# Reading the second layer's expert tokens by indirect transfers and fp32 transposes instead of one-hot matmuls

## The chip, the cores and the metric

The kernel runs on one core of one Trainium2 chip. The time is that of one execution on the device, in microseconds (us), from the first to the last instruction on the slowest (here the only) core, with the launch around it. What counts is the median of several executions.

## The reference, cut to what matters

The model is a trunk of two layers over 256 latent and 256 context tokens of 1024 numbers, all in fp32. A layer is a mixing part (state space, attention, matrix memory) and then a mixture of 64 experts. The first layer's experts see all 512 tokens, the second layer's the 256 latent ones. Each token goes to 8 experts, whose outputs are added with a gate:

```
_, top_e = lax.top_k(jnp.where(allowed, biased, -jnp.inf), TOP_K)      # 8 of 64
gate = jnp.take_along_axis(scores, top_e, axis=1)
gate = gate / jnp.sum(gate, -1, keepdims=True) * ROUTED_SCALE
...
def expert_block(acc, blk):
    tok, g, e = blk                       # 128 rows of one expert
    xb = h[tok]                           # the tokens of this expert
    ob = (jax.nn.silu(xb @ w_gate[e]) * (xb @ w_up[e])) @ w_down[e]
    return acc.at[tok].add(ob * g[:, None]), None
...
shared = (jax.nn.silu(h @ sw_gate) * (h @ sw_up)) @ sw_down
return routed + shared
```

w_gate and w_up are 1024 x 256 for each expert, w_down is 256 x 1024. The line `xb = h[tok]` is the one whose carrying out is changed, in the second layer alone. So 256 x 8 = 2048 token rows are read there.

## The kernel before

`moe(l, ...)` runs a layer's experts. `choose` and `route` find each token's experts, sort the experts by their number of tokens (an expert's place in that order is its rank) and leave the experts' numbers in `idt`. `experts` (from L1634 on in the listing) is a generator that walks through *units*. A unit is one or two tiles of 128 rows: kinds B, C and X have two tiles, and the kinds that the end of the stage is made of have one tile shared by several experts (S: four experts with 32 rows each; M: two with 64). Each expert's part of a tile is a segment. Layer 2 has 26 units with 32 tiles, in the fixed order BDMCSMSLXLMSCXDSCSSSMSLMSM.

Weights come through `ring`, 18 slots of 512 KB in layer 2; an expert takes six of them. `load` (L1720, on SyncE's queue) fills a slot as soon as `use` has given it back. A load of an expert without tokens is skipped once the ring has gone round; 12 of 64 experts have none here, and they come late in the order.

For unit i, `experts` emits: `gather(units[i+2])`, `gate_up(unit i)` (8 steps of matmuls `gu`, L1785), the gate function, `transp(units[i+1])`, `down(units[i-1])` (matmuls `dn`, L1798), the turning of the hidden values (`hT`), and `slots(units[i+5])`. A scheduler then sets the order on each engine, so that the transposes of unit i+1 fall among the first `gu` matmuls of unit i.

`slots` builds one-hot matrices `oneh` (token x place in the tile, bf16), and with matmuls over them finds the token number `gi`/`si` and the gate `gc` of every place. `transp` must give `xT`, the tile's tokens with the 1024 numbers along the partitions, in eight blocks of 128 x 128. In layer 1 `gather` reads the rows of the tokens from `fd` in DRAM by one indirect transfer per segment on GpSimd's queue into one of five tiles `xg`, and `transp` turns them by eight fp32 transposes (`tpose`, L290). In layer 2 there is no gather: `parts` (L1452) has split the normalised tokens f into three bf16 parts `fb` per token tile whose sum is f, and `transp` multiplies each part of both token tiles with the one-hot matrix: 2 x 3 = 6 matmuls per block, 48 per tile (L1760).

`down` scales the outputs by the gates into `xo` (4 buffers) and adds them to `Y` in DRAM by an indirect transfer per segment on GpSimd's queue (L1808). As they add to the same memory, each waits until the one before has landed. The last unit is not scattered: `fold` adds it by matmuls. Afterwards `combine` reads Y back (`cat<-Y`) and forms the output.

Of the kernel before, what the change touches and what calls it, by code (L numbers as in the profile page):

```python
# [20 lines left out]
D = 1024  # L21
# [228 lines left out]
class Trunk:  # L250
    def __init__(self, ctx, tc, d, dbg=None):
# [17 lines left out]
        self.x2 = self.dram.tile([NT, D], F32, name="x2d")  # L269
        self.fd = self.dram.tile([TOK[0], D], F32, name="fd")  # L270
        self.Y = [self.dram.tile([TOK[l] + 128, D], F32, name=f"Y{l}") for l in range(DEPTH)]
# [1083 lines left out]
    def post(self, l, cat, pp, mq, fT, sw):  # L1355
# [38 lines left out]
        def norm(at):  # L1394
            i = tiles[at]
            m = 0 if i >= 2 else 1
            xt = xts[i]
            t = pp.tile([128, D], F32, name="pt", bufs=2)
            for n in range(2):
                cs = slice(n * 512, (n + 1) * 512)  # L1400
                v.tensor_tensor(out=t[:, cs], in0=st[at][n], in1=g1[m][:, cs], op=OP.mult)
            sums = pp.tile([128, 2], F32, name="sums", bufs=2)
            v.scalar_tensor_tensor(out=t, in0=xt, scalar=ALPHA, in1=t, op0=OP.mult, op1=OP.add, accum_out=sums[:, 0:1])
            x1 = pp.tile([128, D], F32, name="x1", bufs=2)
            self.ln_rows(x1, t, *self.ln_sums(pp, t, sums[:, 0:1], x1, "p"), gn, bs, accum_out=sums[:, 1:2])
            nc.sync.dma_start(self.x1[l][i * 128:(i + 1) * 128, :], x1)
            f = pp.tile([128, D], F32, name="f", bufs=2)
            nm, rs = self.ln_sums(pp, x1, sums[:, 1:2], f, "p2")
            v.scalar_tensor_tensor(out=f, in0=x1, scalar=nm, in1=sc[m], op0=OP.add, op1=OP.mult)
            v.scalar_tensor_tensor(out=f, in0=f, scalar=rs, in1=sh[m], op0=OP.mult, op1=OP.add)  # L1410
            if not last:
                nc.sync.dma_start(self.fd[at * 128:(at + 1) * 128, :], f)
            st[at] = f
            if at + 2 < len(tiles):
                fetch(tiles[at + 2])
# [13 lines left out]
        nt = len(tiles)  # L1429
        self.fb = {}  # L1430
        self.G, self.pos1 = (mq.tile([128, nt, 64], F32, name=n) for n in ("G", "pos1"))
# [6 lines left out]
        for at in range(nt):  # L1438
# [8 lines left out]
            self.choose(l, at, lg, pp)  # L1447
            if last:
                self.parts(at, st[at], pp, mq)
        return lg, tiles  # L1450

    def parts(self, i, f, pp, mq):  # L1452

        nc, v = self.nc, self.nc.vector
        fb = self.fb[i] = mq.tile([128, 3, D], BF16, name=f"fb{i}")
        r = pp.tile([128, D], F32, name="frest", bufs=2)
        nc.scalar.copy(fb[:, 0], f)
        v.tensor_tensor(out=r, in0=f, in1=fb[:, 0], op=OP.subtract)
        nc.scalar.copy(fb[:, 1], r)
        v.tensor_tensor(out=r, in0=r, in1=fb[:, 1], op=OP.subtract)  # L1460
        nc.scalar.copy(fb[:, 2], r)

# [117 lines left out]
    def slots(self, l, units, rp, mq):  # L1580
# [6 lines left out]
        for u in units:  # L1587
            for t in u["tiles"]:
                segs = t["segs"]
                n, rk, m = len(segs), sorted(x[0] for x in segs), max(x[2] + x[3] for x in segs)  # L1590
                by = slice(rk[0], rk[-1] + 1, rk[1] - rk[0] if n > 1 else 1)
                t["oh"] = oh = rp.tile([128, nt, 128], BF16, name="oneh", bufs=12 if l else 3)
                lot = [segs] if [x[0] for x in segs] == rk and len({x[1:4:2] for x in segs}) == 1 else [[x] for x in segs]
# [98 lines left out]
    def experts(self, l, units, mq, rp, ring, merge):  # L1692
# [41 lines left out]
        def gather(u):  # L1734
            if l:
                return
            for t in u["tiles"]:
# [3 lines left out]
                for (_, _, col, _, cap), si in zip(t["segs"], t["si"]):  # L1741
                    nc.gpsimd.indirect_dma_start(out=x[col:col + cap], out_offset=None, in_=self.fd,  # L1742
                                                 in_offset=bass.IndirectOffsetOnAxis(ap=si[0:cap], axis=0),
                                                 bounds_check=TOK[l] - 1, oob_is_err=False)

        def transp(u):
            for t in u["tiles"]:
                m = t["m"]
                xt = self.xtp.tile([128, 8, 128], F32, name="xT", bufs=4)
                for hh in range(2):  # L1750
                    ps = self.bank("xT")
                    for k in range(4):
                        cs = slice((hh * 4 + k) * 128, (hh * 4 + k + 1) * 128)
                        o = ps[:, k * 128:k * 128 + m]
                        if l == 0:
                            self.tpose(o, t["x"][0:m, cs])
                        else:
                            parts = [(i, z) for i in self.fb for z in range(3)]
                            for at, (i, z) in enumerate(parts):
                                nc.tensor.matmul(o, self.fb[i][:, z, cs], t["oh"][:, i, 0:m], start=at == 0, stop=at + 1 == len(parts))  # L1760
                    o, a = xt[:, hh * 4:hh * 4 + 4, 0:m], ps.rearrange("p (k n) -> p k n", k=4)[:, :, 0:m]
# [157 lines left out]
    def moe(self, l, mq, fT, sw, lg, tiles, spare):  # L1919
# [5 lines left out]
        with ExitStack() as es:  # L1925
            rp = es.enter_context(self.tc.tile_pool(name=f"moe{l}", bufs=1))
            if l == 0:
                self.xg = [rp.tile([128, D], F32, name=f"xg{i}") for i in range(5)]
                for x in self.xg:
                    nc.gpsimd.memset(x, 0.0)  # L1930
            ring = rp.tile([128, 18 if last else 13, 1024], F32, name="ring")
# [101 lines left out]
```

## Time and profile before

| what | value |
|---|---|
| median of 3 runs | 1990.86 us (1983.97 to 1991.81) |
| the profiled execution | 1989.93 us |
| its span, from first to last instruction | 1988.1 us |
| busy in the span: TensorE, VectorE, ScalarE, GpSimd | 91%, 41%, 19%, 23% |
| DMA | 524.16 MB, 264 GB/s on average |
| layer 2's expert matmuls | from 1440.74 to 1947.76 us |

In the page, PE is TensorE, DVE VectorE, ACT ScalarE, POOL GpSimd and SP SyncE. The chain of waits is the work that ended last, followed back from the end; a row of it has its start, its length and what ran (or what was waited for). A DMA share is the mean busy share of the core's 16 DMA engines; it can come out a little over 1. The group of a line gives busy time and the mean length of one instruction; matmuls overlap in the pipeline, so the mean can be longer than the busy time divided by the count.

### The profile page before, as it was taken

The numbers are of one execution on the slowest core, as the hardware profiler recorded it, in microseconds if no ns is written. First come the engines' busy times: TensorE is split into PE (matmuls) and PEld (weight loads), VectorE is DVE, ScalarE is ACT, GpSimd is POOL, SyncE is SP. The second block draws the span as 40 slices with busy tenths as digits, with TensorE's granted clock in tenths as the row PEclk, the third lists the DMA queues.
The fourth block names the chain that finished last, engine by engine and source line by source line (L and its number), as shares of the span: only waits on it lengthen the run. The fifth ranks groups of instructions, "written<-read, shape, count | busy, mean of one in ns | idle before, by whom it ended". The sixth has DMA issues, their size and how long they took to land. (4 is left out here: it accounts for less than half of the span.)

```text
span 1988.1 us, 29110 instructions
## 1 busy us (share of the span) xinstructions
PE 1802.0 (91%) x10161; PEld 851.0 (43%) x10161; DVE 813.2 (41%) x2298; ACT 379.5 (19%) x739; POOL 456.1 (23%) x453
## 2 busy tenths in 40 slices
PE   6998999879999999899997178899899999999992
PEld 2554665523334333233332055665543354433340
DVE  6856664731223432222121598764731222312113
ACT  2245331201111111001111313341301011110000
POOL 3120211232223232332221551002101211111223
PEclk7999999989999999999999588999999999999996
DMA  8442567399999999999997423256499999899672
GB/s 321 140 96 101 178 250 293 116 319 358 298 326 340 360 323 293 386 377 339 344 297 232 163 75 64 75 213 258 182 372 343 398 353 358 304 385 355 234 261 69
DMA packets 153922, 524.16 MB, mean 264 GB/s; under 512 B 28787, under 2 KB 37939, under 8 KB 145068
## 3 DMA queue, kind: packets, MB, share of 16 engines
q1 hardware_dynamic: 135228, 480.36, 65.1%
q0 software_dynamic: 18544, 41.90, 9.5%
q8 instruction: 82, 1.34, 0.3%
q14 instruction: 68, 0.56, 0.1%
HBM read 531.12 MB, written 47.61 MB: 291 GB/s over the span
## 5 line engine op out<-in xcount | busy, mean ns | idle before, releaser
L1785 PE MATMUL gu<-ring,xT 128*32 128x512 f32 (+5 forms) x2896 | 645.7, 602 | 18.2 <-DMA ring<-in_exp_w 17.7
L1785 PEld LDWEIGHTS gu<-ring,xT 128*32 128x32 f32 (+5 forms) x2896 | 193.7, 129 | 399.3 <-issue 321.2
L1798 PE MATMUL dn<-ring,hT 128*32 128x512 f32 (+5 forms) x1448 | 330.0, 597 | 4.8 <-DMA ring<-in_exp_w 4.0
L1808 POOL DMA_INDIRECT Y<-xo,gi x79 | 119.9, 1518 | 610.8 <-DMA Y<-xo,gi 140.5
L1681 DVE TENSOR_TENSOR hh<-gu,sg 128x256 f32<-128x256 f32 (+4 forms) x86 | 36.5, 424 | 523.2 <-ACT sg L1680 503.7
L1798 PEld LDWEIGHTS dn<-ring,hT 128*32 128x32 f32 (+5 forms) x1448 | 103.1, 128 | 183.2 <-issue 155.7
L1808 POOL DMA_INDIRECT Y<-xo,si x66 | 91.0, 1379 | 302.6 <-DMA Y<-xo,gi 217.4
L1803 DVE TENSOR_SCALAR xo<-dn,gc 128x512 f32<-128x512 f32 (+5 forms) x80 | 60.0, 751 | 229.0 <-PE dn L1798 215.6
L1680 ACT ACTIVATE sg<-gu 128x256 f32<-128x256 f32 (+4 forms) x86 | 32.8, 384 | 586.6 <-PE gu L1785 586.3
L443 PE MATMUL pT<-hT,w 128*128 128x512 f32 (+1 forms) x288 | 120.4, 572 | 4.3 <-DMA w<-in_w_mm 2.7
L1760 PEld LDWEIGHTS <-fb 128*128 128x128 bf16 x1536 | 86.3, 99 | 41.9 <-issue 41.9
L1802 ACT ACTIVATE xo<-dn,gc 128x512 f32<-128x512 f32 (+5 forms) x80 | 55.0, 687 | 253.3 <-PE dn L1798 239.2
L1760 PE MATMUL xT<-oneh,fb 128*128 128x128 bf16 (+4 forms) x1536 | 94.6, 220 | 0.0
L1392 PE MATMUL yo<-w,cat 128*128 128x512 f32 x192 | 83.4, 594 | 0.8 <-DMA w<-in_w_out 0.8
L1762 DVE COPY xT<-xT 128x512 f32<-128x512 f32 (+5 forms) x80 | 53.2, 670 | 70.0 <-PE xT L1760 37.2
L1762 ACT COPY xT<-xT 128x512 f32<-128x512 f32 (+5 forms) x80 | 45.8, 573 | 185.4 <-PE xT L1760 135.3
L443 PEld LDWEIGHTS pT<-hT,w 128*128 128x128 f32 x288 | 56.0, 200 | 58.0 <-issue 47.5
L290 PE MATMUL hT<-cst,xt 128*128 128x128 f32 x64 | 14.6, 404 | 59.3 <-ACT xt L1982 55.2
L451 PE MATMUL pN<-w,hT 128*128 128x256 f32 (+2 forms) x256 | 65.0, 414 | 3.0 <-DVE va L1268 3.0
L342 PE MATMUL ada<-w,sil 128*32 128x512 f32 x384 | 57.9, 649 | 10.4 <-DMA w<-in_ada_w 10.4
L1742 POOL DMA_INDIRECT xg<-fd,gi x48 | 50.3, 1047 | 48.2 <-PE xT L290 19.0
L451 PEld LDWEIGHTS pN<-w,hT 128*128 128x128 f32 x256 | 49.2, 203 | 19.9 <-issue 5.2
(546 smaller groups left out, 2071.1 us busy)
## 6 DMA issues: line engine op xcount, KB each, us to landing
ring<-in_exp_w SPq DMA_DIRECT2D x768, 512.0 KB
w<-in_ada_w SPq DMA_DIRECT2D x48, 1024.0 KB
w<-in_w_out SPq DMA_DIRECT2D x8, 1024.0 KB
sw<-in_sh_w SPq DMA_DIRECT2D x2, 3072.0 KB
w<-in_w_uv SPq DMA_DIRECT2D x4, 1024.0 KB
Y<-zeros SPq DMA_DIRECT2D x8, 512.0 KB
w<-in_w_mm SPq DMA_DIRECT2D x4, 1024.0 KB
w<-in_w_qk SPq DMA_DIRECT2D x4, 768.0 KB
```

The lines of the kernel that those rows point to most:

```text
L342: nc.tensor.matmul(ps[32 * q:32 * q + 32, :], self.sil[:, k, :], t[:, q * 512:(q + 1) * 512], start=k == 0, stop=k == 7, tile_position=(0, ...
L443: self.nc.tensor.matmul(ps[base:base + m, n0:NT], w[k][:, col:col + m], hT[:, k, n0:NT], start=k == 0, stop=k == 7)
L451: self.nc.tensor.matmul(ps[:, :n], hT[:, k, i * 128:(i + 1) * 128], w[k][:, col:col + n], start=k == 0, stop=k == 7)
L1392: nc.tensor.matmul(st[at][n], cb[:, i * 128:(i + 1) * 128], wo[n][b], start=b == 0, stop=b == 7)
L1742: nc.gpsimd.indirect_dma_start(out=x[col:col + cap], out_offset=None, in_=self.fd, in_offset=bass.IndirectOffsetOnAxis(ap=si[0:cap], axis= ...
L1760: nc.tensor.matmul(o, self.fb[i][:, z, cs], t["oh"][:, i, 0:m], start=at == 0, stop=at + 1 == len(parts))
L1762: (nc.scalar.copy if hh else v.tensor_copy)(o, a)
L1785: nc.tensor.matmul(t["gu"][r, :], t["xt"][:, 2 * c + b, r], ws[j][:, b * 512:(b + 1) * 512], start=c == 0 and b == 0, stop=c == 3 and b == ...
L1798: nc.tensor.matmul(po[n][r, :], t["ht"][:, b, r], ws[b * nr + j][:, n * 512:(n + 1) * 512], start=b == 0, stop=b == 1, **kw)
L1802: nc.scalar.activation(xo[0:m, 0:512], po[0][0:m], AF.Identity, scale=t["gc"][0:m])
L1803: v.tensor_scalar(out=xo[0:m, 512:1024], in0=po[1][0:m], scalar1=t["gc"][0:m], scalar2=None, op0=OP.mult)
L1808: nc.gpsimd.indirect_dma_start(out=self.Y[l], out_offset=bass.IndirectOffsetOnAxis(ap=si[0:cap], axis=0), in_=xo[col:col + cap], in_offset ...
```

## The change

Layer 2 does what layer 1 does. f is written to a DRAM tile of its own layer (`fd[l]`), `gather` runs in both layers, the five tiles `xg` exist in both, and `transp` has the transposes alone. `parts` is gone, and `oneh` needs 3 buffers instead of 12.

```diff
-        self.fd = self.dram.tile([TOK[0], D], F32, name="fd")
+        self.fd = [self.dram.tile([TOK[l], D], F32, name=f"fd{l}") for l in range(DEPTH)]
...
-            if not last:
-                nc.sync.dma_start(self.fd[at * 128:(at + 1) * 128, :], f)
+            nc.sync.dma_start(self.fd[l][at * 128:(at + 1) * 128, :], f)
...
             self.choose(l, at, lg, pp)
-            if last:
-                self.parts(at, st[at], pp, mq)
         return lg, tiles
-
-    def parts(self, i, f, pp, mq):
-
-        nc, v = self.nc, self.nc.vector
-        fb = self.fb[i] = mq.tile([128, 3, D], BF16, name=f"fb{i}")
-        r = pp.tile([128, D], F32, name="frest", bufs=2)
-        nc.scalar.copy(fb[:, 0], f)
-        v.tensor_tensor(out=r, in0=f, in1=fb[:, 0], op=OP.subtract)
-        nc.scalar.copy(fb[:, 1], r)
-        v.tensor_tensor(out=r, in0=r, in1=fb[:, 1], op=OP.subtract)
-        nc.scalar.copy(fb[:, 2], r)
...
-                t["oh"] = oh = rp.tile([128, nt, 128], BF16, name="oneh", bufs=12 if l else 3)
+                t["oh"] = oh = rp.tile([128, nt, 128], BF16, name="oneh", bufs=3)
...
         def gather(u):
-            if l:
-                return
             for t in u["tiles"]:
...
-                    nc.gpsimd.indirect_dma_start(out=x[col:col + cap], out_offset=None, in_=self.fd,
+                    nc.gpsimd.indirect_dma_start(out=x[col:col + cap], out_offset=None, in_=self.fd[l],
...
-                        o = ps[:, k * 128:k * 128 + m]
-                        if l == 0:
-                            self.tpose(o, t["x"][0:m, cs])
-                        else:
-                            parts = [(i, z) for i in self.fb for z in range(3)]
-                            for at, (i, z) in enumerate(parts):
-                                nc.tensor.matmul(o, self.fb[i][:, z, cs], t["oh"][:, i, 0:m], start=at == 0, stop=at + 1 == len(parts))
+                        self.tpose(ps[:, k * 128:k * 128 + m], t["x"][0:m, cs])
...
-            if l == 0:
-                self.xg = [rp.tile([128, D], F32, name=f"xg{i}") for i in range(5)]
-                for x in self.xg:
-                    nc.gpsimd.memset(x, 0.0)
+            self.xg = [rp.tile([128, D], F32, name=f"xg{i}") for i in range(5)]
+            for x in self.xg:
+                nc.gpsimd.memset(x, 0.0)
```

On TensorE, at the start of an S unit in the late part of the order, the kernel before has this (`slot` finds the places of a later unit, `dn` is the unit before, `gu` this unit, the rest is the next unit's one-hot work):

```order
L1602 LDWEIGHTS oneh
L1602 MATMUL slot<-tg,oneh 128x10
L1798 MATMUL dn<-ring,hT 32x512 x12
L1785 MATMUL gu<-ring,xT 32x512
L1760 LDWEIGHTS fb_10133
L1760 MATMUL xT<-oneh,fb_10133 128x128
```

The last two rows then follow 48 times in all, with one `gu` matmul somewhere among them, before 30 more `gu`. At the same place the changed kernel has:

```order
L1587 LDWEIGHTS oneh
L1587 MATMUL slot<-tg,oneh 128x10
L1775 MATMUL dn<-ring,hT 32x512 x12
L1762 MATMUL gu<-ring,xT 32x512
L290 MATMUL xT<-cst,xg_10205 128x128 x8
L1762 MATMUL gu<-ring,xT 32x512 x31
```

The 48 matmuls have become eight transposes in one piece, behind the first `gu` matmul, and they read a tile that a gather has filled.

On GpSimd, from the scatters of a two-tile unit to those of an S unit (two thirds through the stage), the kernel before has scatters alone:

```order
L1808 DMA Y_79<-xo,gi 384x1024 x5
L1808 DMA Y_79<-xo,si 384x1024
L1808 DMA Y_79<-xo,gi 384x1024
L1808 DMA Y_79<-xo,si 384x1024 x3
L1808 DMA Y_79<-xo,gi 384x1024 x2
```

In the changed kernel, from the fourth scatter of the first of these rows to the fourth row:

```order
L1785 DMA Y_80<-xo,gi 384x1024
L1725 DMA xg_10204<-fd_78,gi 16x1024
L1725 DMA xg_10204<-fd_78,si 8x1024 x3
L1725 DMA xg_10205<-fd_78,gi 128x1024
L1785 DMA Y_80<-xo,gi 384x1024
L1785 DMA Y_80<-xo,si 384x1024
L1725 DMA xg_10206<-fd_78,gi 80x1024
L1725 DMA xg_10206<-fd_78,si 8x1024
L1725 DMA xg_10207<-fd_78,gi 8x1024
L1725 DMA xg_10207<-fd_78,si 8x1024 x3
L1785 DMA Y_80<-xo,gi 384x1024
L1785 DMA Y_80<-xo,si 384x1024 x3
```

Gathers of later units now stand between the scatters, in the queue's fixed order.

On VectorE, after the first token tile's f, the kernel before has the split between f and the next tile's `pt`:

```order
L1410 SCALAR_TENSOR_TENSOR f<-f,p2rs,sh_9983 128x1024
L1458 TENSOR_TENSOR frest<-f,fb_10133 128x1024
L1460 TENSOR_TENSOR frest<-frest,fb_10133 128x1024
L1401 TENSOR_TENSOR pt<-yo,g_9973 128x512
L1424 COPY fT<-fT 128x4x128
L1403 SCALAR_TENSOR_TENSOR pt,sums<-pxt,pt 128x1024
```

The changed kernel has:

```order
L1410 SCALAR_TENSOR_TENSOR f<-f,p2rs,sh_9984 128x1024
L1401 TENSOR_TENSOR pt<-yo,g_9974 128x512
L1403 SCALAR_TENSOR_TENSOR pt,sums<-pxt,pt 128x1024
L1423 COPY fT<-fT 128x4x128
L393 TENSOR_SCALAR pnm<-sums 128x1
```

The two subtractions are gone, and the copy of the turned f stands one place later.

## Rows read from the trace of the kernel before

**Rows 1.** Busy time by stretch: start:end, length, engines, PEclk, DMA share, GB/s.

```profile
1428.69:1837.50 408.81, 402.52 (x2860) 177.46 (x2861) 108.40 (x384) 44.52 (x81) 62.81 (x44) 1.00 0.96 359
1837.50:1961.60 124.10, 113.84 (x776) 44.23 (x775) 24.34 (x55) 11.51 (x21) 33.43 (x25) 0.97 0.59 209
1580.00:1600.00 20.00, 20.00 (x157) 11.24 (x158) 6.54 (x24) 2.44 (x5) 4.16 (x3) 1.00 1.03 410
...
1860.00:1880.00 20.00, 20.00 (x166) 7.57 (x166) 3.25 (x12) 2.17 (x4) 7.93 (x6) 1.00 0.31 103
```

**Rows 2.** Chain of waits, second expert stretch: first and last step over a load.

```profile
1557.97 9.22 DMA ring<-in_exp_w
...
1818.85 9.79 DMA ring<-in_exp_w
```

**Rows 3.** GpSimd's timeline: start, length, line, operation, count, idle before and releaser.

```profile
1794.60 1.31 POOL L1808 DMA_INDIRECT Y<-xo,gi  x1 [11.66 <-DVE xT L1762]
...
1841.73 1.35 POOL L1808 DMA_INDIRECT Y<-xo,gi  x1 [3.63 <-DMA Y<-xo,si]
1847.27 1.35 POOL L1808 DMA_INDIRECT Y<-xo,si  x1 [4.19 <-DMA Y<-xo,gi]
...
1866.63 1.35 POOL L1808 DMA_INDIRECT Y<-xo,si  x1 [1.59 <-DMA Y<-xo,gi]
1869.57 1.35 POOL L1808 DMA_INDIRECT Y<-xo,si  x1 [1.59 <-DMA Y<-xo,si]
...
1958.45 1.36 POOL L1808 DMA_INDIRECT Y<-xo,si  x1 [1.30 <-DMA Y<-xo,si]
```

**Rows 4.** Chain of waits, end of the second expert stretch.

```profile
1940.53 7.23 PE dn L1798 x32
...
1958.45 2.70 DMA Y<-xo,si
```

**Rows 5.** Groups by line, 1431.84 to 1948: count, busy us, mean ns, idle before.

```profile
L1760 PE MATMUL xT<-oneh,fb 128*128 128x128 bf16 (+4 forms) x1536 | 94.6, 220 | 0.0
```

**Rows 6.** Groups by line, 400 to 1060 (first layer's experts): the transposes.

```profile
L290 PE MATMUL xT<-cst,xg 128*128 128x128 f32 (+4 forms) x376 | 48.2, 273 | 0.0
```

**Rows 7.** Chain of waits, second expert stretch: one-hot and expert matmuls.

```profile
1431.84 6.99 PE xT L1760 x96
...
1522.17 3.57 PE gu L1785 x32
...
1526.18 0.98 PE gu L1785 x2
```

**Rows 8.** DMA queues, 1428 to 1837.5: packets, MB, share of 16 engines.

```profile
q1 hardware_dynamic: 38108, 138.51, 86.0%
q0 software_dynamic: 3344, 7.66, 9.9%
```

**Rows 9.** DMA queues, 398 to 425: gathers of the first layer's start alone.

```profile
q0 software_dynamic: 673, 1.52, 20.1%
```

**Rows 10.** VectorE's timeline between f of the first and work on the second token tile.

```profile
1399.92 1.23 DVE L1458 TENSOR_TENSOR frest<-f,fb 128x1024 f32<-128x1024 f32 x1 [1.17 <-ACT fb L1457]
...
1403.40 0.68 DVE L1401 TENSOR_TENSOR pt<-yo,g 128x512 f32<-128x512 f32 x1
```

**Rows 11.** GpSimd's timeline in the first layer: gathers between two scatters.

```profile
641.46 1.05 POOL L1742 DMA_INDIRECT xg<-fd,gi  x1 [0.30 <-issue]
642.82 0.96 POOL L1742 DMA_INDIRECT xg<-fd,gi  x1 [0.30 <-PE dn L1798]
646.78 1.41 POOL L1808 DMA_INDIRECT Y<-xo,si  x1 [3.00 <-DMA Y<-xo,gi]
```

**Rows 12.** GpSimd's timeline, second layer: scatters of 128 rows under load.

```profile
1762.85 1.48 POOL L1808 DMA_INDIRECT Y<-xo,gi  x1 [9.05 <-ACT xT L1762]
1773.25 1.49 POOL L1808 DMA_INDIRECT Y<-xo,gi  x1 [8.92 <-DMA Y<-xo,gi]
```

**Rows 13.** GpSimd's timeline, first layer: the memsets of xg.

```profile
387.61 4.62 POOL L1930 MEMSET xg<- 128x1024 f32 x5 [10.08 <-PE cnt L1504]
```

More of the change, by code (lines that the diff above doesn't have):

```diff
@@ L1429, in post @@
         nt = len(tiles)
-        self.fb = {}
         self.G, self.pos1 = (mq.tile([128, nt, 64], F32, name=n) for n in ("G", "pos1"))
```

## The prediction

> **What bounds the kernel now.** I read the page for the second layer's expert stretch first, then busy time by stretch, then the chain of waits through it, then GpSimd's own timeline. The reader should see three limits that lie close together, and that they change places.
>
> From 1428.69 to 1837.50 us TensorE is busy 402.52 of 408.81 us, and in the same stretch the 16 DMA engines are busy 0.96 of the time [rows 1]. The most they show is 1.03, in 1580 to 1600 us, where the weight loads run without a break. So TensorE has almost no idle time, and the loads have only 0.07/1.03 of 408.8 us, that is 27.8 us, in hand. The chain says the same: it runs along TensorE, but five times it steps over to a load into the ring (9.22, 10.51, 8.64, 7.87 and 9.79 us, 46 us in all; first and last in [rows 2]). At these places a faster TensorE would only wait for weights.
>
> After 1837.50 most loads are skipped, because the experts that come last in the order hold no tokens; the DMA share is 0.59, and 0.31 in 1860 to 1880 us [rows 1]. The third limit rules there. Each scatter of an expert's output adds to Y in DRAM, and each waits until the one before has landed. On GpSimd's timeline the last break is the 11.66 us ahead of 1794.60; from there on the queue is never empty again [rows 3]. From 1841.73 to the landing of the last scatter at 1961.15 (issued 1958.45, 2.70 us) stand 24 scatters in 119.4 us, 5.0 us each; TensorE's last expert matmuls end at 1947.76 [rows 3, 4]. So the stage ends with the scatters, 13.4 us after TensorE.
>
> **The change, part by part.** *Matmuls removed.* 1536 one-hot matmuls take 94.6 us of TensorE [rows 5]. In their place stand 256 fp32 transposes. The first layer's kernel does the same transposes, 376 in 48.2 us, 128 ns each [rows 6]; 256 x 0.128 = 32.8 us, a saving of 61.8 us, 1.9 us per tile (32 tiles). The mean in that row, 273 ns, is the latency of one instruction in a pipeline; the busy time is what the next instruction waits for. There is a little more: the one-hot matmuls cut expert matmuls of 32 rows off from their neighbours, and two cut off take 0.98 us, where 32 in an unbroken row take 3.57 [rows 7], so a cut loses 0.98 - 2 x 0.112 = 0.76 us. By the order, all eight transposes of a tile now stand together, with one cut per tile instead of two to four; I put it at 0.5 us per tile, as not all tiles have 32-row pieces.
>
> The Trainium skill, "TensorE: Matmul & The Clock Gate", section "Part 4: PE-mode transpose", gives about 275 ns for a 128x128 transpose in a kernel's context. By that the 256 would cost 70 us and only 24 us would be saved; the trace has the same 273 ns as a latency and 128 ns as busy time, so I do not charge 275.
>
> *Where the 62 us go.* Not to the end. Up to 1837.50 the loads have 27.8 us in hand, and the gathers use the same 16 engines. They bring 2048 rows of 4 KB, 8.4 MB; some 0.92 of them (by the tokens of each expert) belong to units whose work starts before 1837.50, 7.7 MB. Three rows bound the price of a MB: plain loads, 86.0% of 409.5 us for 138.51 MB, 2.54 us [rows 8]; the first layer's gathers, 20.1% of 27 us for 1.52 MB, 3.57 us [rows 9]; the scatters that add, 9.9% for 7.66 MB, 5.3 us [rows 8]. The gather row is nearest, but it is of a stretch in which all engines were full and packets stood in line, and a gathered row is the same 4 KB read as a load's; I take 3.2 us, 24.6 us in all. Bounds: 19.6 and 27.5 us, and 41 us by the scatters. So the loads can end 27.8 - 24.6 = 3.2 us earlier, nothing like 62.
>
> *The head.* The split of f into three bf16 parts goes: three casts on ScalarE and two subtractions on VectorE per token tile. For the first tile the next step on VectorE, at 1403.40, starts right behind the second subtraction, which with the first and the casts between takes up the 3.5 us from 1399.92 [rows 10]; the product that this step reads is there before about 1400.8, so 2.6 us go. The second tile has the same three casts and two subtractions in the way of the copies of its turned f, on the same two engines; 2.4 us there. Together -5.0 us for the choice of experts, and so for the first loads, which wait for the expert numbers. Against it, the first unit's tokens now come from DRAM: 1.0 us to the first gather, two more 1.36 us apart [rows 11], some 7 us to land (a 128-row scatter under load takes 10.4 us from its issue to the next one's [rows 12], but few loads are under way yet), 2.0 of transposes and 0.7 for a copy, 13.4 us, where the one-hot matmuls took 6.99 [rows 7] and TensorE has some 2 us of the shared expert to do meanwhile. So +4 for TensorE's start (0 to +9), but the loads keep their -5. No load is on the chain before 1557.97, so TensorE is last up to there, and pays the 4 us back out of its 1.9 us per tile (about ten tiles). The one-hots are still built (the slots' numbers come from them). f written to DRAM, 1 MB more, lies before the first load, when the engines are idle. The five memsets, 4.62 us on GpSimd in the first layer [rows 13], fall into the choice of experts, where GpSimd has little to do; uncovered they would cost those 4.6 us.
>
> So at 1837.50 the chain through the loads is 5.0 + 3.2 = 8.2 us early.
>
> *The tail.* From there TensorE needs about 2.4 us less for each of the last nine tiles, but it was not last. The scatter queue is the same 24 transfers. It gets shorter only where the DMA engines go quiet sooner: with them idle a step is 2.94 us (1866.63 to 1869.57), under load 5.5 (1841.73 to 1847.27) [rows 3]. Loads and gathers stay the same number; they are only pushed together. Bounds 0 and -9; I take -4. Five gathers stand among these scatters; a gather between two scatters has so far lain within the wait for the landing (1.36 us apart, then 3.00 us of wait left [rows 11]): nothing.
>
> Sum: -5.0 - 3.2 - 4.3 = -12.5 us. The profiled execution took 1989.93 us (span 1988.1), 0.93 less than the median of 1990.86: 1977.4 by it, 1978 by the median. Bounds of the terms: head -5 to 0, loads -8.2 to 0, tail -9 to 0, or -22 to 0.
>
> **The rivals.** *R1, TensorE's gain gets through.* If a gather costs the engines next to nothing beside the loads (it fills gaps) and scatters land quicker, loads end 5 + 27.8 = 33 us early and the tail follows TensorE. For it: 2.94 us for a step with idle engines, and 359 GB/s on average against 410 at most [rows 1, 3]. Against it: 0.96 already counts the engines as busy. About 1958 us.
> The Trainium skill, "DMA: Bandwidth & Descriptors", section "Anatomy of one DMA — SWDGE (gpsimd) path", has 2.0 us fixed per DMA plus bytes at 436 GB/s. By it a step of few rows would be near 2 us, the 24 near 50 us, and the end would follow TensorE, as in R1; the trace has 2.94 us idle and 5.0 us on average, so it does not hold under this load.
>
> *R2, the gathers eat it all.* At the scatters' price they need 41 us against 27.8 in hand: loads end 13.4 us later, less 5 for the head and 4 for the tail, +4: 1995 us; at 3.57 us per MB and no gain in the tail -5. Together 1986 to 1997, no change. Speaks for it: the gathers are indirect too, rows to scattered places, and each needs its indices first.
>
> *R3, slower: the gathers lengthen the serial queue.* In the order, 22 gathers stand from the scatter at 1704.58 on among 42 scatters, up to six between two. If a scatter's step grows by each of them (1.36 us [rows 11]), 22 x 1.36 = 30 us come on top of -12.5: +17, 2008 us; TensorE would then also wait for tokens, since the transposes of the next unit stand right after the first expert matmul of this one. It decides once the queue has no break from there on; before, it has one of 11.66 us [rows 3], which would swallow part. Against it: gathers wait for no landing, and a scatter does.
>
> That the change does not do what it says is excluded by the order: no one-hot matmul on xT is left in it, and 70 gathers are there.
>
> **How the numbers follow.** Forecast 0.48, R1 0.13, R2 0.24, R3 0.15. About 0.5% (10 us) is what a measurement of this kernel can tell from no change. Faster by more than that, below 1981 us: 0.40 of the forecast's 0.48 and 0.12 of R1's 0.13, 0.52; slower, above 2001: 0.15; within: 0.33. The range leaves out about half of R1 below 1958 and some two thirds of R3 above 2001: 1958 to 2001.
>
> **What would show it.** The share of the DMA engines from 1424 to 1830 should be 1.0 or more, and the chain should step over to loads into the ring more often, over 70 us instead of 46. The transposes should show 33 us busy. TensorE's last expert matmul should end 20 us or more before the last scatter lands (13 before), with the scatters 4.5 to 5 us apart. The first expert matmul should start at about 1440, as before. A wait of TensorE for xg other than at the start, or gathers after which scatters come without any wait for a landing, would speak for R3; fewer than 20 us of gathers on the engines, with the loads done by 1815, for R1; engines that show over 1.0 all through and a stage that ends no sooner, for R2. I am wrong altogether if the last scatter does not end the stage.

## The result, and the profile after

The changed kernel takes 2000.87 us in the median of six runs, the kernel before 1989.81 us on the same chip: 1.0058 of it (interval 1.0042 to 1.0074), 11 us slower, where 12 us faster was forecast. Sent again with other variants it came to 1.0066 (1.0042 to 1.0090). Two of its executions were profiled, with spans of 2004.5 us (the first, the slowest of its six) and 1995.9 us (the second, the fastest of its four), against 1988.1 before, so that the differences in the table add up to 16.4 and 7.8 us, with the 11 us between. The span falls into five parts, cut at rows of the timelines: the start of the last step of the first token tile's f on VectorE, the issue of the first weight load, the first gate matmul of the 20th unit (the third of three S units in a row), the issue of the reading back of Y, the end.

| us | before | after, first | after, second | change | forecast |
|---|---|---|---|---|---|
| up to the first tile's f | 1397.5 | 1399.2 | 1396.2 | +1.7, -1.2 | 0 |
| f to the first load | 31.2 | 29.8 | 27.2 | -1.4, -4.0 | -5.0 |
| first load to the 20th unit | 407.0 | 432.1 | 429.4 | +25.1, +22.4 | -3.2 |
| 20th unit to Y read back | 125.5 | 120.8 | 120.7 | -4.7, -4.8 | -4.3 |
| from there to the end | 26.9 | 22.6 | 22.4 | -4.3, -4.5 | 0 |

One part has turned round, the stretch of the loads, and it outweighs everything else. The busy time of that stretch, before and after (columns as in [rows 1], of which the row of the whole first stretch answers to these):

```profile
1428.69:1835.70 407.01, 400.72 (x2854) 177.05 (x2856) 108.40 (x384) 43.83 (x80) 62.05 (x43) 1.00 0.97 360
```

```profile
1429.04:1861.10 432.06, 393.31 (x1818) 136.57 (x1819) 108.43 (x384) 44.16 (x81) 127.78 (x109) 0.98 1.00 358
```

TensorE is spared work (1036 matmul records fewer: 29.2 us of transposes in this stretch for 77.2 us of one-hot matmuls), yet the stretch is 25 us longer, the share of the DMA engines is 1.00 instead of 0.97, and TensorE now has 39 us of idle time instead of 6. The idle time tells only a part of the waiting: the same `gu` and `dn` matmuls, now with waits between them, show 345.0 us busy instead of 312.7. The queues of the same two stretches (packets, MB, share; the answer to [rows 8]), before:

```profile
q1 hardware_dynamic: 38108, 138.51, 86.5%
q0 software_dynamic: 3342, 7.66, 10.0%
```

After:

```profile
q1 hardware_dynamic: 38108, 138.51, 84.9%
q0 software_dynamic: 7676, 15.96, 15.2%
```

The loads are the same 138.51 MB in both, so a share times its length, the time that packets held the engines, can be compared: the loads took 0.865 x 407.0 = 352.1 us of the engines before and 0.849 x 432.1 = 366.8 after, scatters and gathers together 40.7 before and 65.7 after. So 8.3 MB of gathers cost 25.0 us, 3.0 us per MB, and the loads beside them 14.7 us more than before.

The chain of waits after, where [rows 2] had two of five rows: now load after load, 34.4% of 553 us or 190 us in all, against 46.

```profile
1526.02 14.93 DMA ring<-in_exp_w
...
1548.54 14.33 DMA ring<-in_exp_w
1562.89 13.75 DMA ring<-in_exp_w
...
1839.13 13.64 DMA ring<-in_exp_w
```

The transposes, by line (the answer to [rows 5] and [rows 6]), are 35.3 us busy for 94.6 us of one-hot matmuls, and TensorE's idle time ahead of them is two single waits, for the two tiles of the first unit:

```profile
L290 PE MATMUL xT<-cst,xg 128*128 128x128 f32 (+4 forms) x256 | 35.3, 284 | 9.5 <-DMA xg<-fd,gi 7.2 <-DMA xg<-fd,si 2.3
```

### The profile page after: what moved, and what is told of

Read it like the earlier page. It is cut to its first block, busy times and chain, and to the rows that moved or that the text cites. A ratio compares the mean times of both kernels' runs of the same rounds, so it can differ in the third digit from the quotient of the medians.

```text
span 2004.5 us, 26807 instructions
## 1 busy us (share of the span) xinstructions
PE 1786.4 (89%) x8881; PEld 801.4 (40%) x8881; DVE 808.3 (40%) x2294; ACT 373.6 (19%) x733; POOL 529.6 (26%) x528
## 4 chain that ended last, share of the span: by engine, by line
PE 49%; DMA 21%; DVE 6%; issue 2%; POOL 1%; ACT 1%; SPq 0%; POOLq 0%; ACTq 0%; DVEq 0%
PE gu L1762 22%; DMA ring<-in_exp_w 15%; PE dn L1775 11%; DMA Y<-xo,gi 3%; PE xT L290 2%; PE gu L1619 2%; PE pT L443 1%; PE yo L1392 1%; DMA Y<-xo,si 1%; PE dn L1634 1%; PE hT L290 1%; PE ada L342 1%; PE o L903 1%; PE s L882 1%; DVE cmB L487 1%
## 5 line engine op out<-in xcount | busy, mean ns | idle before, releaser
L1762 PE MATMUL gu<-ring,xT 128*32 128x512 f32 (+5 forms) x2896 | 657.3, 606 | 37.5 <-DMA ring<-in_exp_w 37.3
L1775 PE MATMUL dn<-ring,hT 128*32 128x512 f32 (+5 forms) x1448 | 353.4, 597 | 7.9 <-DMA ring<-in_exp_w 4.6
L1785 POOL DMA_INDIRECT Y<-xo,gi x79 | 120.7, 1528 | 491.1 <-DMA Y<-xo,gi 122.9
L1775 PEld LDWEIGHTS dn<-ring,hT 128*32 128x32 f32 (+5 forms) x1448 | 107.8, 128 | 205.9 <-issue 167.4
L1665 ACT ACTIVATE sg<-gu 128x256 f32<-128x256 f32 (+4 forms) x86 | 32.8, 383 | 655.2 <-PE gu L1762 632.1
L1725 POOL DMA_INDIRECT xg<-fd,gi x80 | 82.5, 1032 | 116.8 <-DVE gc L1607 38.6
L290 PEld LDWEIGHTS xT<-cst,xg 128*128 128x128 f32 (+5 forms) x640 | 70.0, 142 | 64.2 <-issue 57.3
L290 PE MATMUL xT<-cst,xg 128*128 128x128 f32 (+5 forms) x640 | 84.6, 278 | 9.5 <-DMA xg<-fd,gi 7.2
L1725 POOL DMA_INDIRECT xg<-fd,si x67 | 64.7, 966 | 20.4 <-issue 17.1
```

The source lines that it names most:

```text
L290: self.nc.tensor.transpose(out, in_, self.c("ident")[:in_.shape[0], :in_.shape[0]])
L1762: nc.tensor.matmul(t["gu"][r, :], t["xt"][:, 2 * c + b, r], ws[j][:, b * 512:(b + 1) * 512], start=c == 0 and b == 0, stop=c == 3 and b == ...
L1775: nc.tensor.matmul(po[n][r, :], t["ht"][:, b, r], ws[b * nr + j][:, n * 512:(n + 1) * 512], start=b == 0, stop=b == 1, **kw)
L1785: nc.gpsimd.indirect_dma_start(out=self.Y[l], out_offset=bass.IndirectOffsetOnAxis(ap=si[0:cap], axis=0), in_=xo[col:col + cap], in_offset ...
```

## The experiments

Theory A: the gathers' bytes cost DMA time, their own and that by which they slow the loads. Rival B: GpSimd's serial queue, the forecast's R3. Rival C: the delay of the first unit. A run is given as its ratio to the kernel before on the same chip, with its interval; the changed kernel has 1.0058 or 1.0066.

**Gathers without their bytes.**

```diff
-        self.fd = [self.dram.tile([TOK[l], D], F32, name=f"fd{l}") for l in range(DEPTH)]
+        self.fd = [self.dram.tile([TOK[l], D if l == 0 else 64], F32, name=f"fd{l}") for l in range(DEPTH)]
...
-                    nc.gpsimd.indirect_dma_start(out=x[col:col + cap], out_offset=None, in_=self.fd[l],
+                    nc.gpsimd.indirect_dma_start(out=x[col:col + cap] if l == 0 else x[col:col + cap, 0:64], out_offset=None, in_=self.fd[l],
```

> The changed kernel, but each gathered row of the second layer is 256 bytes instead of 4096 (f's first 64 numbers), so that the experts compute on wrong tokens; every gather, its place in GpSimd's queue, every wait and every transpose stay. Theory A (the gathers' bytes cost the 16 DMA engines about 40 us: 25 of their own and some 15 because the loads' packets get slower beside them): 2000.9 - 25 to 35 = 1966 to 1976 us, and the loads end before 1840 in the trace. Theory B (the 70 gather instructions and their landings stretch GpSimd's serial queue, or TensorE waits for them): no change, 1996 to 2005 us. Theory C (what is lost is lost at the head, where the first unit waits for its tokens): 3 to 6 us faster, because seven small gathers land sooner, 1995 to 1998 us.

0.9895 (0.9867 to 0.9923), 1971.75 us: 1.6% under the changed kernel, near 32 us. The busy time of the stretch from the first load to the 20th unit, and its queues:

```profile
1427.13:1822.90 395.77, 378.14 (x1820) 134.53 (x1820) 108.50 (x384) 44.22 (x81) 124.89 (x106) 0.99 1.00 372
```

```profile
q1 hardware_dynamic: 38108, 138.51, 89.0%
q0 software_dynamic: 5352, 8.16, 10.8%
```

The stretch is 36 us shorter than in the changed kernel's first profile (34 than in the second), with every gather and transpose in its place. The loads are back at 0.890 x 395.8 = 352.2 us. That is theory A, at the upper end of its figure (25 to 35 us); B and C fall for this stretch. (f's own way to DRAM is narrower too here; the next run leaves it whole.) The row also shows what the forecast had not: the engines stand at 1.00 here, and the stretch, rid of gather bytes and of 47 us of TensorE in it, is only 11.2 us shorter than before. That is all that this much TensorE time brought out of the loads, not 27.8.

**Gathers left out, but for the first two units.**

```diff
                 t["x"] = x
+                if l and u is not units[0] and u is not units[1]:
+                    continue
```

> The changed kernel without the gathers of all units but the first two in the second layer (the transposes turn what is left in the five buffers, so the experts compute on wrong tokens). Theory A: within 5 us of the run with narrow rows, but with the head's delay left, so 1968 to 1980 us. Theory B: 15 to 30 us faster than the run with narrow rows, since over 60 instructions of 1.3 us go from GpSimd's queue. Theory C: no change against the changed kernel.

0.9893 (0.9861 to 0.9924), 1971.98 us, and 396.7 us for the stretch: the same as with narrow rows. So 65 instructions on GpSimd's queue, 1.3 us each, and their waits cost nothing that can be measured (each interval is some 6 us wide to either side), where theory B asked for 15 to 30. R3 was not the mechanism.

**No gathers for the first two units.**

```diff
                 t["x"] = x
+                if l and (u is units[0] or u is units[1]):
+                    continue
```

> The changed kernel without the gathers of the first two units (302 of 2048 rows; these units compute on zeros). The first expert matmul should start some 10 us sooner, near 1440. Theory C: 10 us or more faster, 1985 to 1991 us. Theory A: what the head lost is lost in a stretch where the loads set the pace, so a part remains only: 302 rows of the gathers' 40 us are 6 us, plus 0 to 3, 1992 to 1995 us. Theory B: no change over 3 us, as the head has no scatters.

1.0021 (1.0005 to 1.0036), 0.4% under the changed kernel, 7 us. The first gate matmul starts 12.2 us after the first load (1438.55 us by the trace) instead of 22.6 (1451.68), 10.4 us sooner, and a good part of it is gone by the 20th unit: the stretch is 425.1 us, 7.0 less than in the first profile, 4.3 less than in the second. Theory A, with 6 us for these 300 rows, is near; C promised 10 or more, which the intervals of the two ratios don't exclude, so this run alone does not part the two.

**One-tile units by gathers, the rest by one-hots.** Units of one tile with two or four experts have 17 of 32 tiles, but 467 of 2048 rows.

```diff
+def few(u):
+    return len(u['ranks']) >= 2 and len(u['tiles']) == 1
...
-            if l:
+            if l and not few(u):
                 return
...
-                        if l == 0:
+                        if l == 0 or few(u):
                             self.tpose(o, t["x"][0:m, cs])
```

> The kernel before, but units of one tile with two or four experts (S, M and D: 18 of 32 tiles, 467 of 2048 rows) take their tokens by gathers and transposes; the others keep the one-hot matmuls and the three parts. Two buffers for gathered rows, fewer for one-hots, ring of 18 slots as before. Theory A: the gathers cost 467/2048 of 40 us, 9 us of DMA, where 27.8 us are in hand, and TensorE is spared 18 x 1.9 to 2.4 us, 34 to 43 us, of which the loads and the scatters let 5 to 15 through: 1975 to 1985 us, faster than both. Theory B: some 50 gathers remain in GpSimd's queue, most of them in its crowded second half, so no faster than before: 1988 to 1998 us. Theory C: like before in the head, so 1985 to 1990 us.

1.0356 (1.0319 to 1.0394), where theory A had 1975 to 1985 us, faster than both kernels. This says nothing on the theories: in making room I had cut the buffers of the index tiles from 8 to 6 in both layers, and VectorE then waited for scatters to give them back, already in the first layer, where the waits (engine, line, us in total, times, longest) are

```profile
DVE gi L1625 <- DMA Y<-xo,gi: 260.6, 24, 28.4
```

a wait that comes once in the kernel before, for 2.5 us. With the 8 buffers back (and 5 buffers for the other units' one-hots instead of 6):

> The mixed form again: units of one tile with two or four experts (18 tiles, 467 of 2048 rows) by gathers and transposes, the rest by one-hot matmuls; index tiles keep their 8 buffers. Theory A (bytes of the gathers): 467/2048 of 29 us, 7 us of DMA, and TensorE is spared 34 us, mostly in stretches where the loads or the scatters set the pace: 5 to 12 us faster than the kernel before on the same chip. Rival (the loads set the pace so far that TensorE's time is worth nothing there): within 4 us of the kernel before. Rival (the gathers of small units, most of them late, lengthen GpSimd's queue): 5 us or more slower.

1.0016 (1.0003 to 1.0029), 3 us slower than before. The stretch from the first load to the 20th unit:

```profile
1434.22:1845.40 411.18, 395.24 (x2373) 157.22 (x2375) 108.38 (x383) 43.77 (x80) 105.80 (x88) 0.99 0.99 361
```

411.2 us against 407.0. By its queues' shares (86.9% and 11.5%) the gathers cost 6.6 us and the loads 5.2 us more: even 467 rows take nearly what was in hand. Part of the 3 us is the head: the first load comes 35.1 us after f here, 3.9 later than before, with a granted clock of 0.67 in 1416 to 1424 us where it was 1.00 before (below). Theory A's 5 to 12 us did not come; the first rival of this run named the right time, within 4 us, but its reason, that TensorE's time is worth nothing there, does not hold (the runs with fewer parts below).

**Plain transfers in place of the indirect ones.**

```diff
-                for (_, _, col, _, cap), si in zip(t["segs"], t["si"]):
+                for r, base, col, _, cap in t["segs"] if l else ():
+                    k = max(0, min(cap, ROWS[r] - base))
+                    if k:
+                        nc.gpsimd.dma_start(x[col:col + k], self.fd[l][base:base + k])
+                for (_, _, col, _, cap), si in zip(t["segs"], () if l else t["si"]):
```

> The changed kernel, but each gather of the second layer is a plain transfer of as many consecutive rows of fd as the segment has tokens (numbers of rows fixed from these inputs; the experts compute on wrong tokens), on the same queue of GpSimd: the same 2048 rows of 4 KB in the same places, and no list of indices. If the 29 us that the bytes cost are the bytes alone (2048 rows at 159 ns over 16 engines, 20.4 us, and loads unslowed), then like the changed kernel, 1995 to 2003 us, with loads' packets as slow as there. If a part comes from the indirect form (rows fetched one by one at scattered places, with indices read first), the direct form is faster by that part, 5 to 15 us: 1986 to 1995 us, and the loads' packets near 165 ns.

1.0033 (1.0020 to 1.0046). The stretch and its queues:

```profile
1427.30:1852.40 425.10, 390.08 (x1820) 137.74 (x1820) 108.30 (x384) 44.15 (x81) 92.74 (x98) 0.98 1.01 364
```

```profile
q1 hardware_dynamic: 38108, 138.51, 84.9%
q0 software_dynamic: 6800, 15.97, 15.5%
```

The rows cost 65.9 us with the scatters, as before (65.7), and the loads 360.9 instead of 366.8 (364.6 in the second profile). So the indirect form adds 4 to 6 us to the loads, and by the ratios 5 to 7 us to the whole. How much of that is the first unit, which has no indices to wait for here and whose first gate matmul starts at 1439.65 us, 10 us sooner against the first load, is not shown. Loads slow down beside plain transfers too, by 8.8 us.

**Rows farther apart.** fd's rows 16 KB apart, indices times four.

```diff
+                    v.tensor_scalar(out=g8[r, k:e], in0=gi[r, k:e], scalar1=4.0, scalar2=None, op0=OP.mult)
...
-            nc.sync.dma_start(self.fd[l][at * 128:(at + 1) * 128, :], f)
+            w8 = 1 if l == 0 else 4
+            nc.sync.dma_start(self.fd[l].rearrange("(t a) d -> t a d", a=w8)[at * 128:(at + 1) * 128, 0], f)
```

> The changed kernel with the rows of the second layer's fd 16 KB apart instead of 4 KB (3 MB of zeros between them are written at the kernel's start, some 8 us of DMA there), to see whether packets slow down beside gathers because all gathered rows lie within 1 MB of DRAM. If so, packets of loads and gathers in the stretches with gathers go from 220 to 285 ns down towards 160 ns, and the expert stretch is 5 to 15 us shorter than in the changed kernel's profile. If not, the stretch is within 4 us of it.

One execution, 2001.27 us; the stretch is 431.6 us, the loads 0.846 x 431.6 = 365.1 us. Both lie within some 2 us of the changed kernel's two profiles, so, as far as one execution tells, it is not that the gathered rows lie close together.

**Half the bytes.** As in the first experiment, with 512 numbers in place of 64.

> The changed kernel with gathered rows of 2048 bytes (f's first 512 numbers; the experts compute on half of each token). If the cost is in proportion to the bytes, half of the 29 us between the changed kernel and the run with narrow rows comes back: 12 to 17 us faster than the changed kernel, 1984 to 1989 us. If it hangs on the number of rows or instructions, 0 to 5 us faster; if only on rows that fill a whole packet, 25 us or more.

0.9947 (0.9929 to 0.9964): 1.2% under the changed kernel, 23 us of the 32, more than the 12 to 17 for a cost in proportion to the bytes. The stretch is 408.7 us:

```profile
q1 hardware_dynamic: 38108, 138.51, 87.2%
q0 software_dynamic: 6240, 11.76, 12.7%
```

Scatters and gathers together are at 51.9 us, so the gathers at 11.2; the loads are at 356.4 us, 4.3 more than before instead of 14.7 (12.5 in the second profile). The gathers' own time went down with the bytes, and what they add to the loads went down by more than half. How the second part goes with the bytes can't be read from these runs: the 467 whole rows of the mixed run added 5.2 us for 1.7 MB, against 4.3 for 4.1 MB here, and between the runs with few or no gathered bytes the loads' time differs by up to 4 us (348.0 to 352.2).

**The changed kernel once more.**

> The changed kernel once more, for a second profile beside the variants. 1.0058 of the kernel before by what is known (1.004 to 1.008), about 2002 us on a chip where that takes 1991; a stage that is about 15 us longer than before rather than the 19 of the first profile, whose execution was 5 us above the median.

1.0066 (1.0042 to 1.0090); its parts are in the table above. The load stretch is 22.4 us longer than before rather than 25.1, and the head 2.7 us shorter than in the first profile, for a reason told below.

**Less TensorE work and no bytes.** The kernel before, with two parts of f (and in a second run one) in place of three, which leaves out the last bits of f (in the second run all behind the first eight or so) and one or both of VectorE's subtractions in the head.

```diff
-                            parts = [(i, z) for i in self.fb for z in range(3)]
+                            parts = [(i, z) for i in self.fb for z in range(2)]
```

> The kernel before with two bf16 parts of f instead of three (f's last bits are left out): 32 one-hot matmuls per tile instead of 48, 31 us of TensorE spared, no byte more for the DMA engines, one cast and one subtraction less per token tile. Theory D (loads, scatters and gathers together hold the 16 engines at a share of 1.00 at best; before they stand at 0.964, so 14.7 us are in hand and no more): 8 to 15 us faster than before, 1976 to 1983 us. Theory of the prediction (27.8 us in hand): up to 20 us faster. Rival (TensorE's time is worth nothing in this stage): within 4 us.

0.9946 (0.9929 to 0.9962), 1978.6 us, 11.9 under the kernel before: faster than both kernels.

```profile
1422.51:1824.10 401.59, 391.41 (x2446) 157.46 (x2447) 109.99 (x385) 44.47 (x82) 62.84 (x44) 0.99 0.98 365
```

> The kernel before with f rounded to one bf16 part: 16 one-hot matmuls per tile, 63 us of TensorE spared, as much as in the changed kernel, and no byte more. Theory D: hardly more than with two parts, since the 14.7 us are used up: 15 to 22 us faster than before (the head is 5 us shorter too), like the changed kernel with narrow rows. Theory of the prediction: 28 us or more faster. Rival: within 4 us of the kernel before.

0.9897 (0.9869 to 0.9925), near 21 us under the kernel before, like the run with narrow gathers and within the 15 to 22 expected; the forecast's 27.8 us in hand would have made it 28 or more.

```profile
1426.70:1816.00 389.30, 375.44 (x2026) 136.32 (x2026) 107.31 (x384) 44.14 (x81) 62.87 (x44) 0.99 1.00 376
```

With 22.8 us less of one-hot matmuls on TensorE in this stretch it is 5.4 us shorter at a share of 0.98; with 47.8 us less it is 17.7 us shorter at 1.00. My expectation that the second half of the saving is worth hardly anything was wrong (its loads ran a little quicker as well, 0.894 x 389.3 = 348.0 us); that the share ends at 1.00 held. Of the 13.2 us by which the two-part profile is shorter than the one before, another 4.1 are the head. The mixed run had 22.1 us less on TensorE in its stretch, much like two parts, and 11.8 us more on the DMA engines: -5.4 + 11.8 = +6.4 us by this estimate, +4.2 measured.

## Why the prediction was wrong

*What held.* The limits were named rightly: loads up to the late S units, scatters behind. The transposes cost 35.3 us (32.8 forecast), so 59 of the 62 us saved on TensorE are there. By the Trainium skill's figure for a transpose ("TensorE: Matmul & The Clock Gate", "Part 4: PE-mode transpose") they would have been 70 us, an estimate. The trace has about that figure as the mean length of one (284 ns), but 138 ns of busy time for each, so the estimate does not hold here. The gathers' own price was nearly right, 3.0 us per MB for 3.2 forecast, and as gathers run two units ahead it was 8.3 MB rather than 7.7 that fell into the stretch. The last scatter still ends the stage: GpSimd's timeline there (the answer to [rows 3]) has steps of about 3 us with idle engines and 4.5 to 7 under load, and the last scatter is issued at

```profile
1864.56 1.36 POOL L1785 DMA_INDIRECT Y<-xo,gi  x1 [5.56 <-ACT xT L1739]
1869.03 1.35 POOL L1785 DMA_INDIRECT Y<-xo,si  x1 [3.11 <-DMA Y<-xo,gi]
...
1891.03 1.35 POOL L1785 DMA_INDIRECT Y<-xo,si  x1 [1.82 <-DMA Y<-xo,gi]
1894.04 1.32 POOL L1785 DMA_INDIRECT Y<-xo,si  x1 [1.66 <-DMA Y<-xo,si]
...
1979.52 1.33 POOL L1785 DMA_INDIRECT Y<-xo,si  x1 [1.32 <-DMA Y<-xo,si]
```

and Y is read back 17.9 us behind TensorE's last expert matmul (1964.0) where it was 13.4; 20 or more was forecast.

*The tail* came out at -4.7 us where the sum has -4.3 (its text says -4), but that is luck. The forecast wanted shorter steps of the queue, because the engines would go quiet sooner. The steps are as long as before: 25 scatters in the 125.5 us, 24 in the 120.8 and in the 120.7, 5.0 us each in all three. The missing one has only changed sides of the cut, as TensorE comes later to its 20th unit (1835.70 before, 1861.10 after) while the queue goes on. Before and after:

```profile
1836.74 1.35 POOL L1808 DMA_INDIRECT Y<-xo,si  x1 [5.70 <-DMA Y<-xo,gi]
```

```profile
1854.45 1.34 POOL L1785 DMA_INDIRECT Y<-xo,si  x1 [6.82 <-DMA Y<-xo,gi]
```

From this scatter to the reading back of Y it is 124.5 us before, 127.5 and 124.2 after; from the first load to it 408.1 before, 425.4 and 425.9 after. So at the queue, which ends the stage, the stretch of the loads costs 17 to 18 us rather than 22 to 25, and the tail gives nothing.

*The step that failed* is "27.8 - 24.6 = 3.2 us", the loads in the stretch up to 1837.50, in both of its terms. The first: 27.8 us in hand came from the peak of 1.03 in one stretch of 20 us. Over 390 to 430 us all kernels that are bound by loads stand at 0.99 to 1.01; from 0.965 (the sum of the two queues' shares before) to 0.998 (narrow gathers) there are 407.0 x (1 - 0.965/0.998) = 13.5 us. The rows by 40 us tell why. The engines do hold 1.03 for longer than 20 us, but before there are stretches (0.95 and 0.79 below) in which the chain of waits runs along TensorE alone, and only a part of these fills up when TensorE is relieved. Before:

```profile
1500.00:1540.00 40.00, 40.00 (x282) 15.21 (x282) 6.02 (x15) 3.01 (x6) 5.68 (x4) 1.00 0.95 335
1700.00:1740.00 40.00, 40.00 (x278) 18.50 (x271) 16.27 (x48) 4.39 (x8) 8.94 (x6) 1.00 0.79 279
1740.00:1780.00 40.00, 40.00 (x275) 15.30 (x274) 7.92 (x30) 3.62 (x6) 5.84 (x4) 1.00 1.03 381
```

With narrow gathers, where the chain still runs along TensorE's expert matmuls from 1500 to 1527.85 us:

```profile
1500.00:1540.00 40.00, 40.00 (x233) 13.33 (x226) 8.23 (x22) 4.39 (x8) 9.48 (x7) 1.00 0.95 330
1700.00:1740.00 40.00, 40.00 (x246) 15.89 (x248) 13.09 (x46) 6.25 (x11) 12.12 (x10) 1.00 1.02 384
1740.00:1780.00 40.00, 37.90 (x197) 11.31 (x190) 9.14 (x34) 3.70 (x7) 13.27 (x12) 1.00 1.03 381
```

The second: the gathers' price counted their own time alone, and they add 14.7 us (12.5) to the loads. With both mended, -13.5 + 25.0 + 14.7 = +26.2 us, measured +25.1; for the second profile -13.5 + 24.1 + 12.5 = +23.1, measured +22.4; for narrow gathers -13.5 + 2.0 + 0.1 = -11.4, measured -11.2. These sums are no test of their own: both prices are shares of the same stretches, and with the engines at 1.00 the packets' time is the length. That the bytes are the cause is shown by the runs that took them away and gave the loads their 352 us back. The upper bound that the forecast kept, the scatters' 5.3 us per MB, gave 41 us; own time and slowdown together are 39.7 us. I had taken the lower value on the ground that a gathered row is "the same 4 KB read as a load's", which is nearly true of its own time (3.0 us per MB against 2.54). The slowdown could have been read beforehand. In the window of [rows 9] weight loads ran beside the gathers:

```profile
q1 hardware_dynamic: 1778, 6.47, 70.1%
```

That is 0.701 x 27 / 6.47 = 2.92 us per MB against 2.54, 2.5 us more for 1.52 MB of gathers; with their own 3.57, a MB of gathers cost 5.2 us there. (The engines were busy 0.91 of that window, not full all through as the forecast has it.)

*The head.* -5.0 us came out as -1.4 and -4.0. The steps went as forecast up to the logits, then the same eight matmuls of the shared expert stood ahead of the routing at two clocks (below). The second profile had the granted clock of the kernel before there, 1.00, so -4.0 is the change itself.

*The first unit* waited longer than the +4 of the forecast (0 to +9): its first gate matmul came 52.6 us (first) and 49.1 us (second) after f, where it was 43.3, and against the first load 10 to 11 us later than before. It was to be paid back on TensorE before the first wait for a load; that did happen (the lag behind the kernel before was 11 us at the first unit and 2 us at the fifth), but since the loads were bound all the while, what the gathers took from them there came back as later waits.

*The rivals.* R2, "the gathers eat it all", is what happened, and its 41 us were near (39.7), though they are not the gathers' own price but in good part what the loads lost; nor was the indirect form the reason, as the plain transfers show. With 13.5 us in hand in place of 27.8 it ends on the slower side. (Its "13.4 us later" should read 13.2, 41 less 27.8.) R3 named the right direction for the wrong reason: it fell with the two runs without bytes and without gathers. R1 asked that scatters land quicker; with gathered rows of 256 bytes TensorE ended some 21 us sooner, and the stretch from the 20th unit to the reading back of Y still took 127 us. By the fit of the Trainium skill ("DMA: Bandwidth & Descriptors", "Anatomy of one DMA — SWDGE (gpsimd) path") 24 scatters would need about 50 us, an estimate. It does not hold here either.

## What to carry to other kernels

Where two resources stand near their limit, work moved from one to the other must be paid out of what the other can reach over the whole stretch, not in its best 20 us; here 13 us, and gathers of 1.7 MB beside 146 MB cost 12 of them. A transfer's price is its own time and what it adds to the transfers beside it, so take the price from a row of the same mixture, and where rows differ by a factor of two keep the higher one as a case. To make time on the busy engine worth something, take away work without adding bytes: two bf16 parts instead of three, at the price of f's last bits, gave 0.5%; no form of the gathers with whole rows gave anything.

## What the hardware showed that I had not expected

**Loads slow down beside gathers.** In 1440 to 1452 us, with gathers of the first units among the loads, the engines are as busy as in the kernel before and move two thirds of the bytes. Before:

```profile
1440.00:1452.00 12.00, 12.00 (x45) 3.80 (x43) 4.20 (x27) 0.59 (x1) 0.00 (x0) 1.00 1.03 419
```

After:

```profile
1440.00:1452.00 12.00, 7.16 (x27) 4.89 (x28) 2.44 (x6) 1.44 (x3) 1.60 (x2) 0.54 1.04 275
```

It depends on the bytes (half of them, a third of the effect, with some 4 us of doubt on each figure), little on the indirect form, and by one execution not on the distance between the rows. Its cause stays open; a gather into other places of SBUF, or from SBUF, was not tried.

**One program, two clocks.** The same eight matmuls of the shared expert took, in the first profile of the changed kernel,

```profile
1419.03 6.04 PE L1619 MATMUL gu<-sw,fT 128*128 128x512 f32 x8
```

and in the second

```profile
1415.07 3.68 PE L1619 MATMUL gu<-sw,fT 128*128 128x512 f32 x8
```

The granted clock in 1416 to 1424 us was 0.57 in the first and 1.00 in the second and in the kernel before (1.00 is 2.4 GHz, 0.5 is 1.2 GHz). In both, TensorE had been idle for 1.47 us ahead of f's transposes 4.4 us (first) and 3.4 us (second) earlier, so what made the clock fall in the one and not in the other stays open. Over eight profiles of the changed kernel and its variants the first load comes 27.2 us after f where the clock was 1.00 there (four of them) and 29.8 to 30.1 where it was 0.57 to 0.71 (four). So some 2.7 us of a time vary from run to run in this program, a quarter of the difference that was to be explained.

**The end got shorter.** From the reading back of Y to the end it is 22.4 to 22.8 us in the profiles of all kernels that gather through the whole second stage, and 26.8 to 27.1 in those of the four that don't (the kernel before, two parts, one part, no gathers behind the first two units). The arithmetic there is the same; the rest is GpSimd's closing instruction at the end of the program, 9.9 us before and 5.7 after. The forecast had nothing here, and without these 4.3 us the changed kernel would have been slower still. What makes it shorter was not tried.
